# A hybrid conv and gating layer on one core: PE in the program's order, the convolution norm spread over the next units, the second half's input loaded later

## The chip, the core and the metric

The kernel runs on one core of a Trainium2 chip. The core has five engines with queues of their own: PE (TensorE, matrix products), DVE (VectorE), ACT (ScalarE), POOL (GpSimd) and SP (SyncE, which here only issues DMAs). ACT and POOL issue DMAs too, in line with their other work. The metric is the device time of one execution in microseconds.

## The reference

One layer on 2048 tokens of width 1024, in float32, cut to what matters here:

```python
h = rmsnorm(x, g_pre) * (1.0 + scale) + shift      # shift, scale, gate = c @ w_ada + b_ada
p = h @ w_in                                       # 8 column blocks of 1024
a = val * sigmoid(glu)                             # branch A
y = causal_depthwise_conv(a, conv_w, 31 taps) + conv_b
y = silu(layernorm(y, ln_g, ln_b)) * silu(z)       # norm over the 1024 channels
y_a = y @ w_conv_out
v = layernorm(gelu(v))                             # branch B
s = tril(w_s) mixes v in chunks of 128 positions, + bias
y_b = (gelu(u) * s * silu(z_b)) @ w_sgu_out
merged = sigmoid(g_a) * y_a + sigmoid(g_b) * y_b
out = rmsnorm(x + gate * (merged @ w_o), g_final)
```

## The kernel before, in words

The 2048 tokens are done in two halves of 1024 (`for s in range(NS)`, L590), each as two quarters of 512 tokens. Channels lie on the 128 partitions, tokens along the free dimension, except in the v pass and the last product, where it is the other way round. Every product with a weight matrix is made of three float32r matmuls, from operands split into a high and a low part (`split`, L84: an ACT copy gives the high part, a DVE or POOL subtraction the low one; `prod`, L289). Weight pieces are loaded by SP (`raw`), added up where needed and split, four pieces ahead of their use (`take`, L283).

The stages of a half:

- First half only: a part in which PE, DVE, ACT and POOL keep the program's order (`tc.manual_schedule(engines=MANUAL)`, L462 to L564). It computes the token rstd (column sums with `col_sums`, then `spread`), the conditioning `mod` from the wada loads (`ada`), and the first v pass. `load_xn(0, 1, xn)` (L528) loads the second quarter's tokens; wsT and sbias (L566 to L575) are the mixing weights and bias.
- The v pass of both quarters (`v_pass`, L443) with the position mixing (`mixing`, L422). Beside it `halves_sums` (L365) makes four sums or differences of the quarters per channel tile on DVE, which `split` turns into S1, S2, S4 and S3.
- 28 column groups (`quad`, L646). Each makes four blocks of two column tiles by two quarters with seven instead of eight products, of 12 matmuls each, in the order A11, A12, S1, S2, S4, S3, A22; A22 is put off until the next group's A11 is done (`pending`). Copies on ACT and subtractions on DVE link them: S4 adds to a bank that ACT has to copy first, A22 to one that DVE has to read first. Per channel tile there are three groups, for GLU (`glu`), for u and z (`uz`) and for the merge gates (`spilled`, Sigmoid); four more at the end (`spilled`, Silu) give the SiLU gate, stored to d_sz. The convolution of a tile (30 taps on DVE, `convolve`) is put in a list `bg`, and `run_bg(n)` takes n pieces from it at a lower priority.
- The product of branch B (`std_pairs(yb, done_b)`): 16 units of 24 matmuls. After each unit `done_b` multiplies the result with a loaded gate tile gl and stores it to d_mb. Between the units `run_bg(4)` takes four pieces: the token statistics of the next half (`token_stats`), and then the norm of the convolution: `mean` (two channel sums on PE), 16 steps of `centre` (two DVE operations and an ACT square), `ln_rstd` (column sums, root, `spread`, copy), and 16 steps of `conv_out` (scale, SiLU, times a loaded tile zl, split into ya).
- The product of branch A (`std_pairs(ya, done_a)`), which adds up the branches, and the output product (`out_half`, `finish_last`). In the first half the rstd spread and the inputs of the next half are made here, from `bg` (`next_rstd`, `make_h`).

Outside the manual part a scheduler lays out each engine's order ahead of time from its own model of the durations: it takes, of the instructions whose inputs are ready, the one with the lowest priority number, and the number grows along the program (`run_bg` adds LATER = 800). On the chip each engine then keeps that order. Tiles come from pools of fixed size: 28 large tiles (`hs`), six of 512 columns (`t512`), three for loads (`ld`: gl, zl, xs, rl, bl), six PSUM banks.

The change and the steps that speak of it touch the lines named here; the pieces of `bg` that it replaces are these:

```python
for h in range(2):
    bg.append(lambda h=h: mean(h))
for h in range(2):
    bg.extend(lambda h=h, j=j: centre(h, j) for j in range(KT))
    bg.append(lambda h=h: ln_rstd(h))
for h in range(2):
    bg.extend(lambda h=h, j=j: conv_out(h, j) for j in range(KT))
```

Of the kernel before, what the change touches and what calls it, by code (L numbers as in the profile page):

```python
# [7 lines left out]
F32 = mybir.dt.float32  # L8
F32R = mybir.dt.float32r
BF16 = mybir.dt.bfloat16  # L10
AF = mybir.ActivationFunctionType
# [9 lines left out]
T = 512  # L21
# [19 lines left out]
def hybrid_layer(  # L41
# [99 lines left out]
    def col_sums(val, pt, first, n):  # L141

        for c in range(n):
            nc.tensor.matmul(
                pt[:, first + c : first + c + 1], val[:, c * P : (c + 1) * P], one,
                start=True, stop=True,
            )
# [130 lines left out]
    def prep_to(n):  # L278
        while state["prep"] < min(n, len(order)):
            ready.append(order[state["prep"]]())  # L280
            state["prep"] += 1
# [82 lines left out]

    def halves_sums(xn, k):  # L365

        a11, a21 = xn[k][:, :T], xn[k][:, T:S]
        a12, a22 = xn[k + KH][:, :T], xn[k + KH][:, T:S]
        tt = nc.vector.tensor_tensor
        tt(out=a22, in0=a21, in1=a22, op=ALU.subtract)  # L370
        tt(out=a21, in0=a11, in1=a21, op=ALU.subtract)
        tt(out=a11, in0=a22, in1=a11, op=ALU.subtract)
        tt(out=a12, in0=a12, in1=a11, op=ALU.add)
        return a22, a11, a12, a21

# [86 lines left out]
    with tc.manual_schedule(engines=MANUAL):  # L462
# [20 lines left out]
        pc = bank()  # L483
        col_sums(acc, pc, 0, NC)
        prx = spread(rstd_cols(pc[:, :NC], NC), pc)
        rx = t512("rx")
# [15 lines left out]
        shifted(0)  # L502
        prep_to(2)
        cvt = wide()
# [9 lines left out]
        for k in range(KT):  # L514
# [6 lines left out]
            if k + 1 < KT:  # L521
# [4 lines left out]
                shifted(k + 1)  # L526
            if k == 2:
                load_xn(0, 1, xn)  # L528
            if k >= 4:
# [35 lines left out]

    wsT = row("wsT")  # L566
    nc.sync.dma_start(out=wsT, in_=wst.rearrange("p j t -> p (j t)"))
    sbias = hs32("sbias")
    nc.sync.dma_start(out=sbias, in_=rows[:, 2 * D : 3 * D].broadcast_to([P, D]))
    ws3 = wsT.rearrange("p (j t) -> p j t", t=P)  # L570
# [17 lines left out]

    gate_done = None
    for s in range(NS):  # L590
        last = s + 1 == NS
# [26 lines left out]

        pts = v_pass(A[1], mix_first)
        sums4 = [halves_sums(xn, k) for k in range(KH)]  # L620
        S1 = []
        for k in range(KH):
            S1.append(hs("s1"))
            split(S1[k], sums4[k][0])
        v_half(pts, vn1, st1, 1)
# [4 lines left out]
        rest = []  # L630
        for i in (1, 2, 3):
            group = []
            for k in range(KH):
                t = hs("s2")
                after(t[:, 0, 0:1], came)
                split(t, sums4[k][i])
                group.append(t)
            rest.append(group)
# [164 lines left out]

        for j in range(KT):
            glu(j)
            uz(j)
            spilled(AF.Sigmoid, d_sa[j], d_sbg[j])
        for i in range(KH):
            spilled(AF.Silu, d_sz[2 * i], d_sz[2 * i + 1])
        pending.pop()()  # L810
        run_bg(len(bg))


        yb = [[], []]
        for h in range(2):
            for j in range(KT):
                t = hs("yb")
                nc.sync.dma_start(
                    out=t.bitcast(F32).rearrange("p s c -> p (s c)"), in_=d_yb[j][h]
                )  # L820
                yb[h].append(t)

        pmu = []
        rsq = []
        ya = [[None] * KT, [None] * KT]

        def mean(h):
            pmu.append(sums(s1[0][:, h * T : (h + 1) * T]))

# [16 lines left out]

        def ln_rstd(h):
            hh = slice(h * T, (h + 1) * T)
            pc = bank()
            col_sums(rsq[0][:, hh], pc, 0, NC)  # L850
            pr = spread(rstd_cols(pc[:, :NC], NC), pc)
            nc.scalar.activation(rsq[0][:, hh], pr, AF.Copy)

# [9 lines left out]

        if not last:
            rs_next = []
            for h in range(2):
                ss, sq = token_stats(s + 1, h)
                bg.extend(sq)
                bg.append(lambda ss=ss, h=h: rs_next.append(token_rstd(ss, f"rsn{h}")))
        for h in range(2):  # L870
            bg.append(lambda h=h: mean(h))
        for h in range(2):
            bg.extend(lambda h=h, j=j: centre(h, j) for j in range(KT))
            bg.append(lambda h=h: ln_rstd(h))
        for h in range(2):
            bg.extend(lambda h=h, j=j: conv_out(h, j) for j in range(KT))

        def std_pairs(rhs, done):

            for q in range(4):  # L880
                ws = [[take(), take()] for _ in range(2)]
                for h in range(2):
                    for c in range(2):
                        pt = bank()
                        prod(pt, ws[c], rhs[h])
                        done(2 * q + c, h, pt)
                        run_bg(4)

        def done_b(j, h, pt):
            g = load(d_sbg[j][h], "gl")  # L890
            nc.vector.tensor_tensor(out=g, in0=pt, in1=g, op=ALU.mult)  # L891
            nc.gpsimd.dma_start(out=d_mb[j][h], in_=g)  # L892

        std_pairs(yb, done_b)
        run_bg(len(bg))

# [234 lines left out]
```

## Time and profile before

| what | us |
|---|---|
| median of 3 runs | 1947.18 (1946.78 to 1950.36) |
| the profiled execution, its own time | 1949.32 |
| its span, first to last instruction | 1947.6 |
| PE busy | 1859.1 (95%) |
| DVE busy | 1290.7 (66%) |
| ACT busy | 867.6 (45%) |
| POOL busy | 859.9 (44%) |

The mean granted clock of TensorE is 0.98 over the span. A busy share is a mean over stages with different limits; in the column groups PE is busy all the time, DVE mostly with taps and POOL with weights, and in the norm none of them is.

### The profile page before, as it was taken

The numbers are of one execution on the slowest core, as the hardware profiler recorded it, in microseconds if no ns is written. First come the engines' busy times: TensorE is split into PE (matmuls) and PEld (weight loads), VectorE is DVE, ScalarE is ACT, GpSimd is POOL, SyncE is SP. The second block draws the span as 40 slices with busy tenths as digits, with TensorE's granted clock in tenths as the row PEclk, the third lists the DMA queues.
The fourth block names the chain that finished last, engine by engine and source line by source line (L and its number), as shares of the span: only waits on it lengthen the run. The fifth ranks groups of instructions, "written<-read, shape, count | busy, mean of one in ns | idle before, by whom it ended". The sixth has DMA issues, their size and how long they took to land.

```text
span 1947.6 us, 23204 instructions
## 1 busy us (share of the span) xinstructions
PE 1859.1 (95%) x8116; PEld 1517.4 (78%) x8116; DVE 1290.7 (66%) x1636; ACT 867.6 (45%) x1396; POOL 859.9 (44%) x734
## 2 busy tenths in 40 slices
PE   6798999999999998889999999999999999899998
PEld 4577888888888886668888878888888888677886
DVE  6776898888888127475851578889888861845424
ACT  4645555555546435322611455554555453532102
POOL 0035777777777710000100477777777774000000
PEclk9899999999999998889999999999999999899999
DMA  9562332222334384387886332333322246536484
GB/s 331 174 238 92 109 114 100 101 87 92 114 103 146 132 328 137 107 292 243 330 308 220 120 141 75 105 114 103 114 92 97 77 141 253 173 111 198 132 331 169
DMA packets 139015, 313.66 MB, mean 161 GB/s; under 512 B 15889, under 2 KB 16017, under 8 KB 138898
## 3 DMA queue, kind: packets, MB, share of 16 engines
q1 hardware_dynamic: 108434, 237.03, 36.2%
q0 software_dynamic: 11888, 41.43, 5.5%
q10 hardware_dynamic: 18576, 33.73, 4.6%
q8 instruction: 63, 1.03, 0.2%
q14 instruction: 54, 0.44, 0.1%
HBM read 226.66 MB, written 85.46 MB: 160 GB/s over the span
## 4 chain that ended last, share of the span: by engine, by line
PE 74%; issue 11%; DMA 7%; DVE 4%; ACT 3%; POOL 2%; SPq 0%; POOLq 0%; ACTq 0%; DVEq 0%
PE bank L297 21%; PE bank L300 21%; PE bank L303 21%; PE bank L312 3%; PE bank L313 3%; PE bank L314 3%; DMA wo<-d_wo 1%; PE bank L426 1%; DVE wa L387 1%; POOL whl L88 1%; DMA raw<-in_w_v 1%; DMA wa<-in_wada 1%; DMA xn<-in_xt 1%; DMA whl<-d_wo 1%; POOL raw L224 1%
## 5 line engine op out<-in xcount | busy, mean ns | idle before, releaser
L88 POOL TENSOR_TENSOR whl<-raw,whl 128x512 fp32r<-128x512 f32 x392 | 512.8, 1313 | 335.3 <-ACT whl L87 331.1
L704 DVE SCALAR_TENSOR_TENSOR cv<-a,vec,cv 128x1024 f32<-128x1024 f32 x464 | 596.6, 1286 | 31.6 <-ACT cv L698 21.4
L87 ACT ACTIVATE whl<-raw 128x512 fp32r<-128x512 f32 x504 | 314.3, 627 | 414.1 <-PE bank L303 214.7
L300 PE MATMUL bank<-s,whl 128*128 128x512 f32 x896 | 349.3, 390 | 1.7 <-DVE s L88 1.7
L303 PE MATMUL bank<-s,whl 128*128 128x512 f32 x896 | 349.7, 390 | 0.0
L297 PE MATMUL bank<-s,whl 128*128 128x512 f32 x896 | 349.4, 390 | 0.0
L224 POOL TENSOR_TENSOR raw<-raw 128x512 f32<-128x512 f32 x224 | 290.3, 1296 | 17.2
L297 PE MATMUL bank<-h,whl 128*128 128x512 f32 x672 | 264.0, 393 | 0.3 <-ACT bank L657 0.2
L300 PE MATMUL bank<-h,whl 128*128 128x512 f32 x672 | 261.8, 390 | 0.0
L303 PE MATMUL bank<-h,whl 128*128 128x512 f32 x672 | 261.6, 389 | 0.0
L300 PEld LDWEIGHTS bank<-s,whl 128*128 128x128 f32 x896 | 168.6, 188 | 38.0 <-DVE s L88 3.0
L297 PEld LDWEIGHTS bank<-s,whl 128*128 128x128 f32 x896 | 168.6, 188 | 34.9
L303 PEld LDWEIGHTS bank<-s,whl 128*128 128x128 f32 x896 | 168.7, 188 | 34.7
L297 PEld LDWEIGHTS bank<-h,whl 128*128 128x128 f32 x672 | 126.1, 188 | 32.5 <-DVE snap L680 5.3
L303 PEld LDWEIGHTS bank<-h,whl 128*128 128x128 f32 x672 | 126.1, 188 | 26.5
L300 PEld LDWEIGHTS bank<-h,whl 128*128 128x128 f32 x672 | 126.2, 188 | 25.6
L88 DVE TENSOR_TENSOR whl<-raw,whl 128x512 fp32r<-128x512 f32 x112 | 75.9, 688 | 96.9 <-ACT whl L87 91.8
L892 POOL DMA_DIRECT2D mb<-gl x32 | 17.3, 541 | 275.0 <-DVE gl L891 264.3
L297 PE MATMUL bank<-ya,whl 128*128 128x512 f32 x256 | 102.6, 401 | 13.8 <-ACT ya L87 10.6
L652 ACT ACTIVATE snap<-bank 128x512 f32<-128x512 f32 x112 | 66.5, 598 | 98.0 <-PE bank L303 98.0
L297 PE MATMUL bank<-yb,whl 128*128 128x512 f32 x256 | 105.4, 412 | 4.2 <-DVE gl L891 3.5
L300 PE MATMUL bank<-ya,whl 128*128 128x512 f32 x256 | 102.6, 401 | 1.4 <-DVE ya L88 1.4
(214 smaller groups left out, 2867.3 us busy)
## 6 DMA issues: line engine op xcount, KB each, us to landing
raw<-in_w_in SPq DMA_DIRECT2D x224, 256.0 KB, 3.0
yb<-yb SPq DMA_DIRECT2D x32, 512.0 KB, 7.6
whl<-d_wo SPq DMA_DIRECT2D x32, 512.0 KB, 4.6
whl<-d_wv SPq DMA_DIRECT2D x32, 512.0 KB, 4.3
xn<-in_xt SPq DMA_DIRECT2D x32, 256.0 KB, 5.4
wa<-in_wada SPq DMA_DIRECT2D x16, 512.0 KB, 6.5
raw<-in_w_v SPq DMA_DIRECT2D x32, 256.0 KB, 4.8
d_wv<-whl POOLq DMA_DIRECT2D x16, 512.0 KB, 6.5
```

Of the source, the lines that this page charges most:

```text
L87: nc.scalar.activation(hi, val, AF.Copy)
L88: eng.tensor_tensor(out=lo, in0=val, in1=hi.bitcast(F32), op=ALU.subtract)
L224: eng.tensor_tensor(out=dst, in0=dst, in1=src, op=ALU.add)
L297: nc.tensor.matmul(pt, wh, h[:, 0], start=start and k == 0, stop=False, skip_group_check=True)
L300: nc.tensor.matmul(pt, wh, h[:, 1], start=False, stop=False, skip_group_check=True)
L303: nc.tensor.matmul(pt, wl, h[:, 0], start=False, stop=k == last, skip_group_check=True)
L312: nc.tensor.matmul(pt, xh, w[:, 0], start=kt == 0, stop=False)
L313: nc.tensor.matmul(pt, xh, w[:, 1], start=False, stop=False)
L314: nc.tensor.matmul(pt, xl, w[:, 0], start=False, stop=kt == KT - 1)
L387: nc.vector.tensor_tensor_reduce(out=wa[i], in0=wa[i], in1=cbc, scale=col(V_GPRE, k) if i else 1.0, scalar=0.0, op0=ALU.mult, op1=ALU.add, ...
L652: nc.scalar.activation(t, pt, AF.Copy)
L704: nc.vector.scalar_tensor_tensor(out=dst, in0=a[:, k : k + S], scalar=col(V_CW, j * TAPS + k), in1=cv[0], op0=ALU.mult, op1=ALU.add,)
```

## The change

It has four parts. From L590 on PE keeps the program's order, too (the other engines are still laid out by the scheduler). The norm of the convolution is no longer in `bg`: the channel sums and all centring steps stand before the last column group (`before_last`), and column sums, spreads and `conv_out` steps stand behind numbered units of branch B's product (`steps`: unit 4q + 2h + c). The second quarter's tokens, wsT and sbias are loaded only after a one-column copy from `mod` into their tiles (`after`), and the first two weight pieces are made ahead of the first spread. The sums of the quarters are made one by one, where each is split, instead of all ahead of S1.

```diff
-    def halves_sums(xn, k):
...
+    def quarters(xn, k):
+        return xn[k][:, :T], xn[k + KH][:, :T], xn[k][:, T:S], xn[k + KH][:, T:S]
+
+    def sum1(xn, k):
+
+        a11, a12, a21, a22 = quarters(xn, k)
+        nc.vector.tensor_tensor(out=a22, in0=a21, in1=a22, op=ALU.subtract)
+        return a22
+
+    def sum2(xn, k):
+        a11, a12, a21, a22 = quarters(xn, k)
+        nc.vector.tensor_tensor(out=a21, in0=a11, in1=a21, op=ALU.subtract)
+        nc.vector.tensor_tensor(out=a11, in0=a22, in1=a11, op=ALU.subtract)
+        return a11
+
+    def sum4(xn, k):
+        a11, a12, a21, a22 = quarters(xn, k)
+        nc.vector.tensor_tensor(out=a12, in0=a12, in1=a11, op=ALU.add)
+        return a12
+
+    def sum3(xn, k):
+        return quarters(xn, k)[2]
...
         col_sums(acc, pc, 0, NC)
+        prep_to(2)
         prx = spread(rstd_cols(pc[:, :NC], NC), pc)
...
         shifted(0)
-        prep_to(2)
...
             if k == 2:
+                for i in range(KT):
+                    after(xn[i][:, T : T + 1], mod[:, 3, 0:1])
                 load_xn(0, 1, xn)
...
     wsT = row("wsT")
+    after(wsT[:, 0:1], mod[:, KT - 1, 0:1])
     nc.sync.dma_start(out=wsT, in_=wst.rearrange("p j t -> p (j t)"))
     sbias = hs32("sbias")
+    after(sbias[:, 0:1], mod[:, KT - 1, 0:1])
     nc.sync.dma_start(out=sbias, in_=rows[:, 2 * D : 3 * D].broadcast_to([P, D]))
...
     gate_done = None
+    ctx.enter_context(tc.manual_schedule(engines={ET.PE}))
     for s in range(NS):
...
-        sums4 = [halves_sums(xn, k) for k in range(KH)]
         S1 = []
         for k in range(KH):
             S1.append(hs("s1"))
-            split(S1[k], sums4[k][0])
+            split(S1[k], sum1(xn, k))
...
-        for i in (1, 2, 3):
+        for sum_of in (sum2, sum4, sum3):
             group = []
             for k in range(KH):
                 t = hs("s2")
                 after(t[:, 0, 0:1], came)
-                split(t, sums4[k][i])
+                split(t, sum_of(xn, k))
...
+        def before_last():
+            for h in range(2):
+                pmu.append(sums(s1[0][:, h * T : (h + 1) * T]))
+            for h in range(2):
+                for j in range(KT):
+                    centre(h, j)
...
-        def ln_rstd(h):
-            hh = slice(h * T, (h + 1) * T)
+        def ln_cols(h):
             pc = bank()
-            col_sums(rsq[0][:, hh], pc, 0, NC)
-            pr = spread(rstd_cols(pc[:, :NC], NC), pc)
-            nc.scalar.activation(rsq[0][:, hh], pr, AF.Copy)
+            col_sums(rsq[0][:, h * T : (h + 1) * T], pc, 0, NC)
+            ln_pc.append((pc, rstd_cols(pc[:, :NC], NC)))
+
+        def ln_spread(h):
+            pc, cols = ln_pc[h]
+            pr = spread(cols, pc)
+            nc.scalar.activation(rsq[0][:, h * T : (h + 1) * T], pr, AF.Copy)
...
+        steps = {
+            1: [lambda: ln_cols(0)], 2: [lambda: ln_spread(0)],
+            3: [lambda: ln_cols(1)], 4: [lambda: ln_spread(1)],
+        }
+        for j in range(KT):
+            steps.setdefault(3 + j, []).append(lambda j=j: conv_out(0, j))
+            steps.setdefault(8 + j, []).append(lambda j=j: conv_out(1, j))
...
         for i in range(KH):
+            if i == KH - 1:
+                run_bg(len(bg))
+                before_last()
             spilled(AF.Silu, d_sz[2 * i], d_sz[2 * i + 1])
         pending.pop()()
         run_bg(len(bg))
...
                         done(2 * q + c, h, pt)
                         run_bg(4)
+                        for step in steps.pop(4 * q + 2 * h + c, ()):
+                            step()
```

What is not shown: the loads of yb stand behind the definitions now, and the token statistics go into `bg` behind them, as its only pieces.

## Rows read from the trace of the kernel before

**Rows 1.** The page, part 1: busy us, share of the span, instructions.

```profile
PE 1859.1 (95%) x8116; PEld 1517.4 (78%) x8116; DVE 1290.7 (66%) x1636; ACT 867.6 (45%) x1396; POOL 859.9 (44%) x734
```

**Rows 2.** PE by stretches: stretch, its length, busy (matmuls), granted clock, DMA share, GB/s.

```profile
200.00:600.00 400.00, 400.00 (x1762) 1.00 0.30 102
722.00:880.00 158.00, 131.68 (x524) 0.89 0.57 183
1655.00:1762.00 107.00, 94.22 (x386) 0.92 0.46 153
```

**Rows 3.** The same two stretches, matmuls that read yb alone.

```profile
722.00:880.00 158.00, 68.50 (x281) 0.89 0.57 183
1655.00:1762.00 107.00, 89.30 (x362) 0.92 0.46 153
```

**Rows 4.** Groups on PE from 722 to 880: count, busy us, mean ns, idle before.

```profile
L144 PE MATMUL bank<-one,rsq 128*128 128x1 f32 x16 | 2.5, 261 | 8.3 <-DVE rsq L843 8.3
L161 PE MATMUL bank<-diag,ones 128*128 128x512 f32 x4 | 2.2, 630 | 2.8 <-ACT q L842 1.4 <-DVE diag L154 1.4
L166 PE MATMUL bank<-s,ones 128*128 128x512 f32 x4 | 1.9, 591 | 0.0
```

**Rows 5.** Waits of PE from 722 to 880: us in total, times, longest.

```profile
PE bank L297 <- ACT ya L87: 10.6, 2, 5.5
PE bank L144 <- DVE rsq L843: 8.3, 2, 6.2
...
PE bank L297 <- DVE gl L891: 1.2, 1, 1.2
```

**Rows 6.** One stretch, all engines: PE, PEld, DVE, ACT, POOL busy, clock, DMA.

```profile
646.00:700.00 54.00, 54.00 (x240) 44.47 (x239) 6.91 (x10) 24.46 (x42) 30.62 (x24) 1.00 0.62 233
```

**Rows 7.** Groups on DVE from 730 to 850: the adding up of squares.

```profile
L843 DVE TENSOR_TENSOR rsq<-rsq,q 128x512 f32<-128x512 f32 x14 | 9.6, 683 | 0.9 <-ACT q L842 0.7
```

**Rows 8.** Timeline of PE and DVE near 695: start us, us, what.

```profile
695.28 0.39 PE L303 MATMUL bank<-s,whl 128*128 128x512 f32 x1
...
695.71 0.69 DVE L680 TENSOR_TENSOR snap<-snap,bank 128x512 f32<-128x512 f32 x1 [1.31 <-PE bank L303]
```

**Rows 9.** Timeline of DVE and POOL near 176.

```profile
175.58 2.78 DVE L88 TENSOR_TENSOR s<-xn,s 128x512 fp32r<-128x512 f32 x2
...
176.51 1.29 POOL L88 TENSOR_TENSOR whl<-raw,whl 128x512 fp32r<-128x512 f32 x1
```

**Rows 10.** Timeline of ACT, PE and DVE in the start.

```profile
20.21 0.81 ACT L352 ACTIVATE h<-xn,mod 128x512 fp32r<-128x512 f32 x1 [0.76 <-DVE xn L492]
...
22.44 0.79 PE L539 MATMUL bank<-whl,h 128*128 128x512 f32 x1 [3.62 <-ACT whl L87]
...
58.69 1.23 DVE L387 CUSTOM_DVE_ANT_0 wa<-wa,cbc 128x1024 f32<-128x1024 f32 x1 [4.02 <-DMA wa<-in_wada]
```

**Rows 11.** Timeline of PE in the v pass.

```profile
108.39 0.50 PE L313 MATMUL bank<-whl,h 128*128 128x512 f32 x1 [2.01 <-DVE whl L88]
```

**Rows 12.** Timeline of PE and ACT in one group of the merge gates.

```profile
326.51 0.39 PE L303 MATMUL bank<-s,whl 128*128 128x512 f32 x1
...
326.72 0.59 ACT L652 ACTIVATE snap<-bank 128x512 f32<-128x512 f32 x1
...
328.55 0.39 PE L297 MATMUL bank<-s,whl 128*128 128x512 f32 x1
```

**Rows 13.** Timeline of PE and DVE where the output product begins.

```profile
918.75 0.80 PE L312 MATMUL bank<-whl,mg 128*128 128x512 f32 x1
...
924.63 0.68 DVE L154 TENSOR_TENSOR diag<-ident,rsn 128x512 f32<-128x512 f32 x1
```

**Rows 14.** DMA issues from 690 to 850: count, KB each, median us to landing.

```profile
mb<-gl POOLq DMA_DIRECT2D x16, 256.0 KB, 3.6
zl<-sz SPq DMA_DIRECT2D x16, 256.0 KB, 2.9
gl<-sbg SPq DMA_DIRECT2D x13, 256.0 KB, 2.8
```

More of the change, by code (lines that the diff above doesn't have):

```diff
@@ L363, in make_h @@
         A[h].append(t)
-    def halves_sums(xn, k):
[L367 to L374, printed above, removed]
+    def quarters(xn, k):
[15 more added lines that the diff above has]
+        return quarters(xn, k)[2]
     def load_ada(k):
@@ L802, in spilled @@
             )
[L804 to L821, printed above, removed]
         pmu = []
@@ L825, in hybrid_layer @@
         ya = [[None] * KT, [None] * KT]
-        def mean(h):
-            pmu.append(sums(s1[0][:, h * T : (h + 1) * T]))
+        ln_pc = []
+        def before_last():
[4 more added lines that the diff above has]
+                    centre(h, j)
         def centre(h, j):
@@ L862, in conv_out @@
             split(ya[h][j], v)
[L864 to L869, printed above, removed]
-        for h in range(2):
[L871 to L876, printed above, removed]
+        steps = {
[5 more added lines that the diff above has]
+            steps.setdefault(8 + j, []).append(lambda j=j: conv_out(1, j))
+        for j in range(KT):
+            glu(j)
+            uz(j)
+            spilled(AF.Sigmoid, d_sa[j], d_sbg[j])
+        for i in range(KH):
+            if i == KH - 1:
+                run_bg(len(bg))
+                before_last()
+            spilled(AF.Silu, d_sz[2 * i], d_sz[2 * i + 1])
+        pending.pop()()
+        run_bg(len(bg))
+        yb = [[], []]
+        for h in range(2):
+            for j in range(KT):
+                t = hs("yb")
+                nc.sync.dma_start(
+                    out=t.bitcast(F32).rearrange("p s c -> p (s c)"), in_=d_yb[j][h]
+                )
+                yb[h].append(t)
         def std_pairs(rhs, done):
@@ L892, in done_b @@
             nc.gpsimd.dma_start(out=d_mb[j][h], in_=g)
+        if not last:
+            rs_next = []
+            for h in range(2):
+                ss, sq = token_stats(s + 1, h)
+                bg.extend(sq)
+                bg.append(lambda ss=ss, h=h: rs_next.append(token_rstd(ss, f"rsn{h}")))
         std_pairs(yb, done_b)
```

## The prediction

> **What bounds the kernel now.** I read the page first: PE is busy 95% of the span [rows 1], so only time in which PE stands still, or runs at its lower clock, can be won. Then PE by stretches [rows 2]: in the column groups from 200 to 600 us it starts 1762 matmuls in 400 us, 0.227 us apart, at a full granted clock. Two stretches are worse: 722 to 880 us, where the convolution norm of the first half lies among the output products, and 1655 to 1762 us, the same place in the second half. Their granted clock is 0.89 and 0.92, between the levels 2.4 GHz (1.00) and 1.2 GHz (0.50), because PE ran part of them at the lower one.
>
> What these stretches cost: the first holds 524 matmuls [rows 2], of which 24 are small work of the norm (16 column sums, 4 spreads, 4 sums of channels) [rows 4] and 500 are products of two units' inputs, 281 of them from yb [rows 3]. 500 x 0.227 = 113.5 us, so 158.0 - 113.5 = **44.5 us** are not product time. The second has 362 yb products [rows 3]: 107.0 - 82.2 = **24.8 us**. The small matmuls themselves are busy 2.5 + 2.2 + 1.9 = 6.6 us [rows 4]. The largest waits say who is late: the first ya tile's copy by ACT, 10.6 us, and the squares' sum on DVE, 8.3 us [rows 5]. The norm is late, not PE.
>
> **Part 1: the norm placed unit by unit.** The two channel sums and all 16 centring steps move ahead of the last column group. Their input is there: between 646 and 700 us DVE is busy 6.9 of 54 us [rows 6], so the taps have ended. A centring step is two DVE operations and one ACT square; a DVE one takes 0.683 us [rows 7], so 16 x 2 x 0.683 = 22 us on DVE, beside the last group's 84 x 0.227 = 19 us of PE. The norm's column sums stand behind units 1 and 3 of yb, the spreads behind units 2 and 4, and a unit is 24 x 0.227 = 5.4 us: the last square sum is due about 22 us after the last group ends, so it is hidden. conv_out (three DVE operations, 2.05 us; two on ACT) comes once a unit, twice in units 8 to 10. With done_b and one weight split that is at most 4.1 + 1.4 = 5.5 us of DVE against 5.4: hidden, without slack in three units. Its zl loads move with it on SP's queue, between the gl loads; in the first half the token statistics' xs loads come behind the yb loads as before.
>
> What stays of 44.5 and 24.8: the 6.6 us of small matmuls in each. New in each: in the program's order the last group's A22 product stands straight behind S3, and it waits for a DVE subtraction; S3's last matmul is over at 695.28 + 0.23, the subtraction at 695.71 + 0.69 [rows 8], so 0.9 us, where four yb products filled the gap. A centring step ahead of it on DVE adds 0.7: I take 1.5. For loads and splits that come late I estimate 3.5 us in the first half and 2.0 in the second (bounds 0, and 15 and 10 if the waits for rsq stay [rows 5]). So 11.6 and 10.1 us stay, and 32.9 + 14.7 = **47.6 us** go.
>
> On that subtraction a row speaks against the move: two DVE splits with both inputs in SBUF took 2.78 us at 175.58, where two take 1.37 by [rows 7], while POOL ran its own at 176.51 [rows 9]. The Trainium skill has the rule (SBUF — State Buffer, "Who interferes with whom"): a DVE instruction with two SBUF inputs and a GpSimd one that reads SBUF block each other for a whole instruction. By it the square sums, now beside POOL's splits of the last group, could put one such block of 1.4 us ahead of the subtraction in each half, and the sum would give 44.8 instead of 47.6; I leave it in the range.
>
> **Part 2: input and sums made later.** The first weight splits move ahead of the spread. PE starts its products at 22.44 us after a wait of 3.62 for the split; ACT's h is done at 20.21 + 0.81 = 21.02 [rows 10], so 1.4 us go. The second half's eight xn loads leave their early place on SP's queue for one behind mod[3]; what stands behind them there are the weights' and wada's loads of the next steps, and eight one-column copies (under 0.15 us each) enter DVE's chain. Early wada loads gain, later ones lose; the wait of 4.0 us at 58.69 for a wada load [rows 10] is not touched. wsT and sbias load after mod[7], with their mask and copies on POOL behind; they are wanted after 128 us. Net **1.5 us** (bounds -4 and +6). The quarter sums leave DVE where it makes PE wait 2.0 us for a weight split at 108.39 [rows 11]; they run in later DVE gaps: **1.0** (bounds 0 and 2, or a loss of 2 if S2 then waits).
>
> **Part 3: PE in the program's order.** 40 of the 56 column groups have that order already, counted in PE's timeline. In 16 groups (8 in each half, those of the merge gates), the old order put matmuls of the next group ahead of S4, mostly 8 [rows 12]: S2 ends at 326.51 + 0.23 and S4 starts at 328.55. In the new order S4 waits there for ACT's copy of its bank, done at 326.72 + 0.59 = 327.31, 0.6 us; everything behind S4 on PE waits too. 16 x 0.6 = 9.6 us (bounds 0, if ACT's order shifts, and 16 x 8 x 0.227 = 29). In the first group of each half the old order filled waits with 15 such matmuls (3 and 12), 3.4 us; I take half, 2 x 1.7 = 3.4 (bounds 0 and 6.8). The rstd spread for the next half moves to behind the first weight tile of out_half: PE is there at 918.75 + 12 x 0.227 = 921.5, the DVE product it needs ends at 924.63 + 0.68 = 925.3 [rows 13], 3.8 us; I take 4 (bounds 1 and 6). Sum **17.0 us** lost.
>
> **Sum.** 47.6 + 1.5 + 1.0 - 17.0 = 33.1. The profiled execution took 1949.3 us (span 1947.6 and 1.7 around it), so 1916.2; the median shown is 2.1 lower, so **1914 us**. A measurement tells about 0.2%, 4 us, from no change.
>
> **Rivals.**
> *Order free.* ACT's order is laid out anew, and S4 never waits: part 3 costs 17.0 - 9.6 - 1.4 = 6, so 1903. For it: 40 groups run so. Against: the copy comes behind ACT's work on the group before, in either order. Chance 0.20.
> *Order in full.* Every matmul that filled a gap covered a real wait: 29 + 6.8 + 6 = 42 instead of 17, so 1939. For it: the gaps were filled where something was expected late. Against: the ACT copy ends after 0.6 us. Chance 0.13.
> *Norm half won.* DVE's queue keeps centring steps and late loads in an order in which PE still waits for rsq: 24 of 47.6, so 1938. For it: the old order expected the squares' sum earlier than it came [rows 5]. Chance 0.13.
> *Slower: the three load tiles bind.* gl, zl and xs share three buffers. A gl tile is held for 2.8 (load) + 0.7 + 0.5 + 3.6 us (store) = 7.6, a zl tile for 2.9 + 2.2 = 5.1 [rows 14]; 16 of each, and 8 xs held like a zl tile (they are read by one ACT operation), make 244 tile-us in the first half, 203 in the second, against 3 x 87 = 261 in a yb pass. It fits, but not if tiles are fetched ahead: x us more for each of the 32 tiles lengthens the passes by (64x - 75)/3, which eats the 33 us at x = 2.7. At x = 4 it is 60 us: 1974. Against: with the same tiles in use, PE waited 1.2 us for gl and 10.6 for ya [rows 5]. Chance 0.06.
> *Forecast* 0.44; 0.04 for the rest (a slower start, more won).
>
> **How the numbers follow.** 1914 is the likeliest case; its own range, from its bounds, is 1904 to 1927. Order free reaches down to 1897, the two at 1938 and 1939 stay in up to 1942; load tiles and tails are left out: **1897 to 1942**. Faster holds all but the load tiles, and small parts of the tails: 0.88, same 0.05, slower 0.07.
>
> **What would show it.** Right: channel sums before the last group's first product, PE's waits for rsq and for ya's copy gone, the two stretches' surplus near 11 us, a PE wait of about 0.6 us before S4 in 16 groups with no matmuls of the next group ahead of it, and one of about 4 us in out_half. Wrong: idle time of PE for gl or for a split during yb (load tiles), a DVE subtraction late by several us in the last group, or a wada wait that grew in the first 80 us.

## The result and the profile after

The changed kernel took 1961.89 us (median, 1959.48 to 1966.23); the kernel before, on the same chip, 1947.26. The ratio is 1.0074, 95% interval [1.0053, 1.0096]: slower by 14.6 us, where 1914 had been forecast, with a range that ended at 1942.

The page of the changed kernel, span and part 1, against [rows 1]:

```profile
span 1957.8 us, 23201 instructions
...
PE 1860.5 (95%) x8116; PEld 1515.8 (77%) x8116; DVE 1300.1 (66%) x1646; ACT 871.6 (45%) x1396; POOL 866.8 (44%) x734
```

The same work on every engine (DVE has ten one-column copies more), in a span 10.2 us longer. That is less than the 14.6 us of the medians: the profiled execution of the kernel before took 1949.32 us and that of the changed one 1959.48, the shortest of its four. Where the time went is read best by stages. A stage ends where PE starts the first product of the next one in the timeline, the last one with PE's last product (7.5 us before the end of the span in both); lengths in us:

| stage | before | after | difference |
|---|---|---|---|
| start, up to the first column group | 148.0 | 155.0 | +7.0 |
| column groups, first half | 547.5 | 575.8 | +28.3 |
| products of yb and ya (the norm), first half | 222.0 | 189.3 | -32.7 |
| output, and v pass of the second half | 185.4 | 191.3 | +5.9 |
| column groups, second half | 545.0 | 567.3 | +22.3 |
| products of yb and ya, second half | 202.6 | 177.9 | -24.7 |
| output of the second half | 89.6 | 93.8 | +4.2 |

In the kernel before, the first products of yb stand ahead of A22, so A22's 12 x 0.227 = 2.7 us count there with the norm and in the changed kernel with the groups. Moved over, the norm's stages gained 30.0 + 22.0 = **52.0 us** and the groups lost 25.6 + 19.6 = **45.2 us**. The rest lost 17.1.

PE by stretches of the changed kernel: a stretch inside the groups, then the two stages of [rows 2] (the second one up to the first ya product). Columns: length, then busy and matmuls of PE, PEld, DVE, ACT and POOL, then granted clock, DMA share, GB/s.

```profile
200.00:600.00 400.00, 396.78 (x1743) 326.38 (x1742) 332.55 (x318) 210.03 (x331) 299.21 (x230) 1.00 0.30 100
730.80:920.00 189.20, 182.38 (x790) 148.02 (x789) 104.83 (x171) 63.17 (x106) 10.83 (x20) 0.98 0.67 219
1678.60:1769.30 90.70, 90.70 (x405) 74.61 (x404) 52.77 (x83) 38.50 (x57) 8.15 (x15) 1.00 0.55 180
```

The granted clock, 0.89 and 0.92 before, is 0.98 and 1.00: the norm's stages are cured. But the groups, which never stood still in [rows 2], now have 1743 matmuls where they had 1762. The waits of PE in the changed kernel say on what (line, releaser: us in total, times, longest):

```profile
PE bank L297 <- ACT snap L668: 23.7, 18, 7.8
PE bank L553 <- ACT h L352: 10.8, 3, 8.2
...
PE bank L161 <- DVE diag L154: 6.5, 2, 3.3
PE bank L297 <- ACT whl L87: 5.8, 3, 4.5
PE bank L297 <- DVE snap L696: 3.9, 3, 2.3
PE bank L312 <- DMA wo<-d_wo: 3.3, 6, 1.5
```

The waits for `rsq` and `ya` of [rows 5] are gone. In their place stand ACT's copy of a bank (`snap`), the modulated tiles of the start (`h`, 4.5 us before), and smaller ones for a spread (`diag`, one in the start and one in the output), for weight splits (`whl`, in the product of branch A) and for the output weights (`wo`).

**The longest copy wait.** Timeline of PE, ACT and DVE in the last group of the first half, changed kernel (start us, us, what, idle before):

```profile
711.35 0.39 PE L303 MATMUL bank<-s,whl 128*128 128x512 f32 x1
719.55 0.80 PE L297 MATMUL bank<-s,whl 128*128 128x512 f32 x1 [7.81 <-ACT snap L668]
...
715.66 0.63 ACT L845 ACTIVATE q<-a 128x512 f32<-128x512 f32 x1 [0.57 <-DVE a L838]
716.86 0.63 ACT L845 ACTIVATE q<-a 128x512 f32<-128x512 f32 x1 [0.57 <-DVE a L838]
717.39 1.07 ACT L804 ACTIVATE sp<-bank 128x512 f32<-128x512 f32 x2
...
718.90 1.08 ACT L668 ACTIVATE snap<-bank 128x512 f32<-128x512 f32 x2 [0.44 <-ACT sp L804]
...
716.09 0.68 DVE L838 SCALAR_TENSOR_TENSOR a<-bank,a 128x512 f32<-128x512 f32 x1
```

S2 ends at 711.6 and S4 waits for the copy of the bank it writes to. That copy stands on ACT behind all sixteen squares of the centring, and each square waits for a DVE subtraction; subtractions and additions take turns on DVE, a pair every 1.2 us. So the copy comes only when the whole chain has run. The second half shows the same wait, 7.8 us at 1666.

**The start.** Timeline of SP's DMA issues, DVE and PE, changed kernel:

```profile
35.00 0.42 SPq L393 DMA_DIRECT2D wa<-in_wada  x1
40.27 5.08 SPq L329 DMA_DIRECT2D xn<-in_xt  x8
45.40 0.59 SPq L393 DMA_DIRECT2D wa<-in_wada  x1
...
40.10 0.57 DVE L92 COPY xn<-mod 128x1 f32<-128x1 f32 x8
...
52.88 1.28 DVE L399 CUSTOM_DVE_ANT_0 wa<-wa,cbc,vec 128x1024 f32<-128x1024 f32 x1 [9.75 <-DMA wa<-in_wada]
...
55.28 0.79 PE L553 MATMUL bank<-whl,h 128*128 128x512 f32 x1 [8.18 <-ACT h L352]
```

The eight loads are those of the second quarter's tokens, `load_xn(0, 1, xn)`; the title, the prediction and some of the expectations call them the second half's input. They wait for the fourth shift and then go out in one piece, between the two tiles of one `wada` pair. Wait of SP's queue from 30 to 50 us:

```profile
SPq L329 <- DVE xn L92: 5.1, 1, 5.1
```

So the held loads kept the queue standing for 5.1 us, with the second `wada` tile in line behind them, and then took 5.1 us to issue. That tile is issued 10 us after the first, and DVE waits 9.75 us for it, where the longest such wait was 4.02 [rows 10].

### The profile page after: what moved, and what is told of

It reads as the page before. It is cut to its first block, busy times and chain, and to the rows that moved or that the text cites. A ratio compares the mean times of both kernels' runs of the same rounds, so it can differ in the third digit from the quotient of the medians.

```text
span 1957.8 us, 23201 instructions
## 1 busy us (share of the span) xinstructions
PE 1860.5 (95%) x8116; PEld 1515.8 (77%) x8116; DVE 1300.1 (66%) x1646; ACT 871.6 (45%) x1396; POOL 866.8 (44%) x734
## 4 chain that ended last, share of the span: by engine, by line
PE 72%; issue 9%; DMA 7%; ACT 5%; DVE 5%; POOL 2%; SPq 0%; ACTq 0%; POOLq 0%; DVEq 0%
PE bank L297 20%; PE bank L303 20%; PE bank L300 20%; PE bank L312 3%; PE bank L314 3%; PE bank L313 3%; DMA wo<-d_wo 1%; PE bank L438 1%; ACT whl L87 1%; ACT L804 1%; DMA zl<-sz 1%; DVE wa L399 1%; DVE cv L720 1%; DMA wa<-in_wada 1%; POOL whl L88 1%
## 5 line engine op out<-in xcount | busy, mean ns | idle before, releaser
L88 POOL TENSOR_TENSOR whl<-raw,whl 128x512 fp32r<-128x512 f32 x392 | 518.6, 1326 | 351.4 <-ACT whl L87 344.1
L720 DVE SCALAR_TENSOR_TENSOR cv<-a,vec,cv 128x1024 f32<-128x1024 f32 x464 | 596.8, 1286 | 31.5 <-ACT cv L714 21.4
L297 PE MATMUL bank<-ya,whl 128*128 128x512 f32 x256 | 101.0, 395 | 5.8 <-ACT whl L87 5.8
L303 PE MATMUL bank<-ya,whl 128*128 128x512 f32 x256 | 101.1, 395 | 1.1 <-DVE whl L88 0.9
L300 PE MATMUL bank<-ya,whl 128*128 128x512 f32 x256 | 100.6, 393 | 0.0
```

What stands on the lines that cost most here:

```text
L88: eng.tensor_tensor(out=lo, in0=val, in1=hi.bitcast(F32), op=ALU.subtract)
L297: nc.tensor.matmul(pt, wh, h[:, 0], start=start and k == 0, stop=False, skip_group_check=True)
L300: nc.tensor.matmul(pt, wh, h[:, 1], start=False, stop=False, skip_group_check=True)
L303: nc.tensor.matmul(pt, wl, h[:, 0], start=False, stop=k == last, skip_group_check=True)
L720: nc.vector.scalar_tensor_tensor(out=dst, in0=a[:, k : k + S], scalar=col(V_CW, j * TAPS + k), in1=cv[0], op0=ALU.mult, op1=ALU.add,)
```

## The experiments

All times are medians; the ratio is to the kernel before, run beside them: 1948.23 us for experiments 1 to 4, 1948.47 for 5 to 8, 1949.24 for 9 to 12. By the intervals of the ratios, a difference between two of these kernels is known to 4 or 5 us. Stages are those of one profiled execution, which can lie 2 us off the median.

**1. The centring in the queue of small steps.**

```diff
 def before_last():
     for h in range(2):
         pmu.append(sums(s1[0][:, h * T : (h + 1) * T]))
     for h in range(2):
-        for j in range(KT):
-            centre(h, j)
+        bg.extend(lambda h=h, j=j: centre(h, j) for j in range(KT))
```

> The changed kernel, with the sixteen centring steps of the convolution norm handed to the queue of small steps (two after each product, the rest behind the last group) where the change issues all of them ahead of the last group; PE's order and all else are as changed. Theory: the two waits of 7.8 us for the copies at L668, with the slower clock behind each, come from fourteen squares that stand ahead of the copy on ScalarE, each waiting for a VectorE subtraction; last group and A22 go from 33.3 and 34.1 us back to 24 to 25, so 14 to 20 us less than the 1961.9 of the changed kernel: 1942 to 1948, likeliest 1945, and the longest wait for a copy is below 2 us. Rival: VectorE's work in the last group is too much in whatever order; the wait turns up at the first products of yb instead (on the norm's sums and its spread), and the gain is 0 to 7 us: 1955 to 1962.

Measured: **1945.9 us**, ratio to before 0.9993 [0.9977, 1.0009]; 16.0 us less than the changed kernel. Waits of PE in this kernel:

```profile
PE bank L297 <- ACT snap L668: 8.3, 16, 1.4
```

The long waits are gone and did not come back at yb; the theory holds. (It is sixteen squares, not fourteen.) So the centring's place cost 8 us in each half. The sixteen short waits in the groups are left.

**2. The changed kernel without the order on PE.**

```diff
-    ctx.enter_context(tc.manual_schedule(engines={ET.PE}))
```

> The changed kernel without the line that holds PE to the program's order; all else as changed. Theory: the order costs what the trace of the changed kernel shows on PE, 0.62 us in each of the sixteen groups and 2 to 4 us in each mixing, first group and output stage, 24 us in all, and outside the order PE also fills part of the two long waits of the last group with products of yb: 22 to 36 us less than 1961.9, so 1926 to 1940, likeliest 1932. Rival: the norm gains only because its small products are held to their units; let free, they stand again where an estimate puts them and the waits for rsq and ya come back, as in the kernel before: 1945 to 1960.

Measured: **1922.34 us**, 0.9872 [0.9851, 0.9892]: 39.6 us less than the changed kernel, a little beyond the theory's 22 to 36. The rival is out: the norm's small products stay with their units and no wait for `rsq` or `ya` returns. The centring still shows; timeline of PE and DVE behind the last group:

```profile
697.71 0.40 PE L300 MATMUL bank<-yb,whl 128*128 128x512 f32 x1
703.33 0.80 PE L303 MATMUL bank<-yb,whl 128*128 128x512 f32 x1 [5.22 <-DVE whl L88]
...
702.00 0.68 DVE L845 TENSOR_TENSOR rsq<-rsq,q 128x512 f32<-128x512 f32 x1
702.60 0.68 DVE L88 TENSOR_TENSOR whl<-raw,whl 128x512 fp32r<-128x512 f32 x1
```

PE passes S4 and goes on to yb, and stops there on a weight split that stands behind the same chain on DVE.

**3. The start as before, in the changed kernel.**

```diff
-        prep_to(2)
         prx = spread(rstd_cols(pc[:, :NC], NC), pc)
...
         shifted(0)
+        prep_to(2)
...
-                for i in range(KT):
-                    after(xn[i][:, T : T + 1], mod[:, 3, 0:1])
...
-    after(wsT[:, 0:1], mod[:, KT - 1, 0:1])
...
-    after(sbias[:, 0:1], mod[:, KT - 1, 0:1])
```

> The changed kernel with the edits to the start undone: no waits ahead of the second half's input, the triangle of weights or the bias, and the first weight split back in its place. Theory: the second half's input, held until the fourth shift is known, then goes to the queue as one burst ahead of a later tile of the modulation's weights, which lands 9.75 us after VectorE asks for it (before: 4.0); undone, the start is 4 to 7 us shorter: 1955 to 1958. Rival: the start is bound by the sum of what it has to load, and a later stage takes up the time: 0 to 2 us, 1960 to 1962.

Measured: **1955.68 us**, 1.0041 [1.0026, 1.0057]: 6.2 us less than the changed kernel, as the theory had it.

**4. The order alone, in the kernel before.**

```diff
     gate_done = None
+    ctx.enter_context(tc.manual_schedule(engines={ET.PE}))
     for s in range(NS):
```

> The kernel before, with nothing added but the line that holds PE to the program's order behind the start. Theory: the groups lose 12 to 14 us in the first half of the sequence and 6 in the second, the output stage 5, and the norm, whose small products are then in line behind VectorE's chain, 0 to 10 more than before: 20 to 35 us slower than 1947.3, so 1967 to 1982. Rival: the waits that the changed kernel's groups show come from its later sums of quarters and from the norm, not from the order: 1947 to 1957.

Measured: **1947.19 us**, 0.9996 [0.9983, 1.0009]: no change. My theory failed here, and its rival's reason fails too, for the stages moved a lot, in both directions: groups +16.4 and +10.8 us, output +7.5 and +6.9, norm **-29.6 and -15.4** (2.7 of each pair is A22, moved over). So the order by itself wins 39.6 us in the norm's stages, and loses as much elsewhere. Why is in the timeline of DVE and PE of the kernel before:

```profile
767.50 0.68 DVE L843 TENSOR_TENSOR rsq<-rsq,q 128x512 f32<-128x512 f32 x1
...
768.24 0.58 PE L144 MATMUL bank<-one,rsq 128*128 128x1 f32 x2 [6.19 <-DVE rsq L843]
...
814.54 0.72 PE L144 MATMUL bank<-one,rsq 128*128 128x1 f32 x6
```

and in the same two engines of this kernel:

```profile
771.57 0.69 DVE L844 TENSOR_TENSOR rsq<-rsq,q 128x512 f32<-128x512 f32 x1
...
778.65 0.95 PE L144 MATMUL bank<-one,rsq 128*128 128x1 f32 x8
```

In both the last sum of squares of the second tile is done by 768 and 772. The program's order takes the eight column sums at 778.65; PE's free order had put two of the eight ahead of their data, where PE stood 6.19 us of the 8.3 for `rsq` [rows 5], and six at 814.54, 46 us behind their data. Spread, multiplication and ya stood behind these: the 10.6 us wait for `ya` [rows 5] was a wait for PE's own late products.

**5. Order, start and centring undone together; the norm's units and the later sums of quarters stay.** The diffs of 1, 2 and 3 in one kernel.

> The changed kernel with three things undone together: no line for PE's order, the start as before, and the centring steps of the convolution norm in the queue of small steps in place of ahead of the last group. What is left of the change is the norm's placing unit by unit and the later sums of quarters. Theory: the three costs are apart from each other. From 1922.3 without the order, 6 us less for the start, and per half 6 to 8 us less for the wait of 5.22 us on a weight split behind the centring on VectorE and for the slower clock behind it: 1898 to 1906, likeliest 1903. Rival: without the order PE already passes what the centring holds up, and the wait only moves on to the norm's sums: 1912 to 1918.

Measured: **1902.12 us**, 0.9763 [0.975, 0.9776]. Theory right; this beats both kernels. Its page and the waits of PE inside the first yb and ya stage:

```profile
PE 1843.8 (97%) x8116; PEld 1508.4 (79%) x8116; DVE 1296.7 (68%) x1636; ACT 864.8 (46%) x1396; POOL 859.4 (45%) x734
```

```profile
PE bank L297 <- ACT whl L87: 4.6, 2, 4.0
PE bank L297 <- DVE snap L691: 1.4, 1, 1.4
PE bank L303 <- DVE xn L92: 0.7, 1, 0.7
```

**6. The same, with the centring ahead of the last group again** (the diff of 1 taken back).

> As the kernel beside it that undoes order, start and centring, but with the centring ahead of the last group as the change has it. Theory: 1922.3 less 6 for the start: 1914 to 1918, and 11 to 16 us behind the kernel beside it. Rival: centring ahead costs only under PE's order: within 3 us of the kernel beside it.

Measured: **1915.94 us**, 0.9832 [0.9819, 0.9845]: 13.8 us behind kernel 5. The centring's place costs under either order, 16.0 with it (experiment 1) and 13.8 without.

**7. Kernel 5 with the sums of quarters at once, as before.**

```diff
+        sums4 = [halves_sums(xn, k) for k in range(KH)]
         S1 = []
...
-            split(S1[k], sum1(xn, k))
+            split(S1[k], sums4[k][0])
...
-        for sum_of in (sum2, sum4, sum3):
+        for i in (1, 2, 3):
...
-                split(t, sum_of(xn, k))
+                split(t, sums4[k][i])
```

> As the kernel that undoes order, start and centring, with the sums of quarters too made at once as before. Theory: the prediction took 1.0 us for making them later; within 2 us of the kernel beside it, on either side. Rival: the sums at once hold VectorE and with it the first products of the groups: 3 to 8 us slower.

Measured: **1903.87 us**, 0.9773 [0.9758, 0.9787], against 0.9763 [0.975, 0.9776]: no difference that these runs can tell. This part is worth 1.8 us at the medians, if anything.

**8. The kernel before with the order over yb and ya alone.**

```diff
-        std_pairs(yb, done_b)
-        run_bg(len(bg))
+        with tc.manual_schedule(engines={ET.PE}):
+            std_pairs(yb, done_b)
+            run_bg(len(bg))
...
-        std_pairs(ya, done_a)
-        run_bg(len(bg))
+        with tc.manual_schedule(engines={ET.PE}):
+            std_pairs(ya, done_a)
+            run_bg(len(bg))
```

> The kernel before, with PE held to the program's order over the products of yb and ya alone, in both halves; groups, mixing, output and start stay free. Theory: the norm's surplus came from where PE's free order put the small products, and either cure takes the whole of it: over these stages the kernel with the order everywhere showed 192.4 us for 222.0 and 187.2 for 202.6, so 45 us less than 1947.3 without the losses elsewhere: 1900 to 1908. Rival: the order's losses elsewhere are the price of the same thing, PE's work being moved across stages, and held here it shows up in the stages beside: 1930 to 1947.

Measured: **1917.88 us**, 0.983 [0.9812, 0.9848]. Between the two: 30.6 us won, two thirds of what I expected. The norm's stages are 199.2 and 190.9 us, 22.8 and 11.7 less than before, 10.5 short of the 45: 5.4 are A22, which counts with the norm here and which I had missed. The first half's output stage is 3.8 us longer. The waits of PE in this kernel show what the placing unit by unit gives beyond the order:

```profile
PE bank L161 <- DVE diag L154: 13.3, 5, 5.1
```

In the old program the spread stands right behind its column sums and PE waits for DVE's diagonal; with a unit's product between the two, kernel 5 shows 1.5 us for all of its spreads, all of it in the start. That is 11.8 of the 15.8 us between kernels 8 and 5.

**9. Kernel 5 with the order over the column groups alone**, and **10. the same with S1's product ahead of A12's.** The edit of 9, then that of 10:

```diff
+        in_order = tc.manual_schedule(engines={ET.PE})
+        in_order.__enter__()
         for j in range(KT):
             glu(j)
...
         pending.pop()()
         run_bg(len(bg))
+        in_order.__exit__(None, None, None)
```

```diff
-            prod(a, [take()], A12, start=False)
-            c11(a)
-            run_bg(2)
             c = bank()
             prod(c, [take()], S1)
             p5 = snap(c)
             run_bg(2)
+            prod(a, [take()], A12, start=False)
+            c11(a)
+            run_bg(2)
...
-            order += [quad_piece(q, k) for k in ("b21", "t1", "t2", "b22", "t3")]
+            order += [quad_piece(q, k) for k in ("t1", "b21", "t2", "b22", "t3")]
```

> The kernel of 1902 us, which undoes order, start and centring, with PE held to the program's order over the column groups alone (mixing of the second tile included). Theory: the order's price lies first in the groups; there the two traces that differ by order and start show 564.5 us for 549.2 in the first half and 560.2 for 547.2 in the second, 28 us, of which 8 are products of yb that the free order had drawn ahead: 1918 to 1931, likeliest 1922. Rival: the prediction's price, sixteen waits of 0.6 us and 3 us for the first group of each half: 1911 to 1917.

> As the kernel beside it with the groups in order, and the product of the first sums (S1) written before that of A12 in each group, so that the copy of its bank has a product more before S4 writes there. Theory: it is not order as such that costs, but this order, in which S4 waits in sixteen groups for a copy that stands behind ScalarE's work for the group before; written so, these waits go: 8 to 14 us less than the kernel beside it. Rival: the wait moves to the next product that needs ScalarE or VectorE in the same group, and nothing is won: within 3 us.

Measured: 9 took **1923.49 us**, 0.9871 [0.985, 0.9892], 21.4 us more than kernel 5; 10 took **1907.97 us**, 0.9797 [0.9777, 0.9818], 15.5 us less than 9. The theory of 9 holds; that of 10 holds in kind, with a gain 1.5 us above its 8 to 14. Waits of PE in 9:

```profile
PE bank L297 <- ACT snap L663: 8.4, 17, 0.8
```

In 10 the copies have no row among PE's waits any more; the largest of its groups' waits is for splits of the sums, of which S1's are wanted one product earlier:

```profile
PE bank L300 <- DVE s L88: 9.1, 11, 2.8
```

So most of the price in the groups is that of one place in the written order, not of an order as such. The 15.5 us are more than the sixteen waits (9.9 us, below): by stages the groups win 14.4 us in the first half and 4.7 in the second, and the norm's stages lose 2.9 and 2.8 of it again. What else is won in the first half's groups was not taken apart.

**11. Kernel 5 with the order over the output stages alone.**

```diff
+        in_order = tc.manual_schedule(engines={ET.PE})
+        in_order.__enter__()
         came = mg[1][KT - 1][:, 1, 0:1].bitcast(F32)
...
         out_half(0)
         out_half(1)
+        in_order.__exit__(None, None, None)
```

The exit stands behind the last half's output too.

> The kernel of 1902 us with PE held to the program's order over the output stages alone (from the merge's end on, in both halves). Theory: this stage pays 7 us in the first half (spread of the next tokens' factor in line behind a VectorE step) and 7 at the end (late output weights, which PE may not pass): 1913 to 1918. Rival: the prediction's 4.0 us for this stage and nothing at the end: 1905 to 1907.

Measured: **1919.06 us**, 0.9848 [0.9826, 0.987]: 17.0 us more, 1 above the theory's range. By stages the first half's output takes 6.4 us more and the last output 8.0, 14.4 in all; the profiled execution is 19.0 us longer than kernel 5's, and the other 4.6 lie in stages that the edit does not touch. Waits of PE in this kernel:

```profile
PE bank L312 <- DMA wo<-d_wo: 4.4, 8, 1.5
...
PE bank L161 <- DVE rx L92: 3.6, 1, 3.6
```

The free order fills the time in which the output weights arrive (0.3 us of such waits in kernel 5); in order, each late tile stops PE.

**12. Kernel 5 with the hold on the second quarter's tokens alone.**

```diff
             if k == 2:
+                for i in range(KT):
+                    after(xn[i][:, T : T + 1], mod[:, 3, 0:1])
                 load_xn(0, 1, xn)
```

> The kernel of 1902 us with one edit of the start put back: the second half's input waits for the fourth shift of the modulation. Theory: this edit alone makes the start longer, by the modulation weights that come behind the burst: 4 to 7 us more, 1906 to 1909. Rival: it is the first weight split, put ahead of the spread of the token factor, or the later triangle and bias, and the hold costs nothing: 1901 to 1904.

Measured: **1910.03 us**, 0.9802 [0.978, 0.9823]: 7.9 us more, 1 above the theory's range. The line of the `wada` reductions (idle time before them), in kernel 5 and then here:

```profile
DMA wa<-in_wada: 6.5, 3
```

```profile
DMA wa<-in_wada: 13.6, 3
```

DVE waits 7.1 us more. The profiled execution is 10.3 us longer than kernel 5's: the start 4.5, the rest in later stages (mostly the first half's norm and output, 2.9 and 2.6), which was not followed further. In the profiled executions with the hold the start takes 152.3 to 158.0 us; in those without it 147.6 to 149.2, but 151.8 in experiment 3. So the hold alone costs as much as all edits of the start together (6.2 to 6.4), as far as these runs can tell.

## Why the prediction was wrong, point by point

Three steps failed: what the centring ahead of the last group costs, what the held loads cost, and the sum of what the order costs. The parts add up. From kernel 5, by its own median: 1902.1, + 13.8 for the centring's place (6), + 6.4 for the start (experiment 2 less 6), + 21.4 and + 17.0 for the order in groups and output (9, 11) make 1960.7; the changed kernel took 1961.9. As each part is known to 4 or 5 us, that it comes out within 1.2 is partly chance.

| part | forecast, us | measured, us | from |
|---|---|---|---|
| norm unit by unit and sums of quarters | -51.6 | -46.3 | kernel 5 against before |
| centring ahead of the last group | +3.0 | +13.8 to +16.0 | 6, 1 |
| start | -1.5 | +6.2 to +6.4 | 3, 2 less 6 |
| order, column groups | +13.0 | +21.4 | 9 |
| order, output | +4.0 | +17.0 (14.4 in its own stages) | 11 |

(The forecast's -47.6 held 1.5 us of loss in each last group; they stand in a row of their own here, and its 1.0 for the sums with the first row.)

**Part 1, the gain: right in size, wrong in cause.** The norm's waits went, and the channel sums stand ahead of the last group's first product. The size was worked out from the surplus of the stretches, so it did not hang on the cause; of its estimate for late loads and splits (3.5 and 2.0 us) the first half shows 6.7 us of PE waiting for weight splits, the second none. But "The norm is late, not PE" was wrong: the sums of squares were done at 768, and PE's free order took their columns at 814 (experiment 4). The prediction read the releaser of ya's wait, ACT, and did not follow it back to PE. Had it done so, it could have seen that the order alone cures most of the same loss (39.6 us, experiment 4). The change pays for two cures of one loss: on the kernel before, the order wins about 40 us in the norm and loses as much elsewhere; beside the norm's units it wins next to nothing, and costs 38 to 40.

**Part 1, the failed step: "A centring step ahead of it on DVE adds 0.7: I take 1.5".** The 22 us of DVE were laid beside 19 us of PE and taken as hidden. They were not beside it but in line: the sixteen squares stand on ACT ahead of the group's copies, and S4 waits for the copy. The step looked at A22, behind S3, and at DVE alone; the wait came two products earlier, on ACT. It is 7.8 us in each half, and 8 us in each by experiment 1. The prediction's list of signs had it ("a DVE subtraction late by several us in the last group"), its sum had not.

**Part 2, the failed step: "Early wada loads gain, later ones lose", with a net gain of 1.5 us and a loss of at most 4.** The prediction saw that the loads behind the moved ones are those of `wada`, and then took the gain of the first split as the likelier end. The hold kept SP's queue standing for 5.1 us and then made 2 MB (eight tiles of 256 KB) one burst, both ahead of a tile that was needed 3 us after the burst began. The wait at 58.69 that it named did stay (3.07 us in the changed kernel); a new one of 9.75 us came ahead of it. The loss of 6.2 to 6.4 us is over the bound of 4. Of the split's 1.4 us nothing came: the first product starts at 23.2 us, not earlier than 22.44 [rows 10]. Moved ahead of the spread, the split's two ACT copies, and a table load of 1.28 us behind them, stand before the root of the token rstd, which starts at 17.44 us where it started at 15.36:

```profile
14.81 1.32 ACT L87 ACTIVATE whl<-raw 128x512 fp32r<-128x512 f32 x2 [2.58 <-DMA raw<-in_w_v]
...
17.44 0.26 ACT L137 ACTIVATE cols<-bank,eps_t 128x4 f32<-128x4 f32 x1
```

**Part 3: the price of one wait right, the sum too small.** S4's wait is as forecast, 0.62 us of lost pitch, 0.46 of it the wait, in each of the groups of the merge gates but the last (16 x 0.62 = 9.9 us):

```profile
222.81 0.59 ACT L668 ACTIVATE snap<-bank 128x512 f32<-128x512 f32 x1
...
223.45 0.50 PE L297 MATMUL bank<-s,whl 128*128 128x512 f32 x1 [0.46 <-ACT snap L668]
```

The eight matmuls of the next group that stood there before [rows 12] are gone. The failed step is "Sum 17.0 us lost": what was mis-sized is all else. The other half of the 21.4, where 3.4 stood, lies nearly all in the first half, whose groups are 14.8 us longer in kernel 9 than in kernel 5 (5.5 in the second half). There PE waits in the first group for splits of the sums (0.58, 1.13 and 1.25 us) and runs behind these waits at a granted clock of 0.52 from 184 to 188 us, where kernel 5 has 1.00. The output cost 17.0, where 4.0 stood for one spread, which alone measured 3.2 us in the changed kernel:

```profile
927.70 1.44 PE L161 MATMUL bank<-diag,ones 128*128 128x512 f32 x2 [3.16 <-DVE diag L154]
```

The last output, where PE may no longer pass late weights, had no term at all. The rival *order in full* (42 us, against 38 to 40) had the size by luck, for another reason: matmuls that filled gaps in the groups.

**The sum.** Short were the gain by 5.3, the centring by 10.8, the start by 7.9, the order by 8.4 in the groups and 13.0 in the output: 45.4 us, and with the 1.3 by which the kernel before stood higher in these runs, 1914 becomes 1960.7. The range took the misses one at a time; five on the same side were in no case of it. The slower rival named the load tiles, and PE's waits in the products of yb and ya show none for them.

**The rule on DVE and GpSimd, weighed in the prediction.** In the last group of the first half four additions of squares took longer than the usual 0.68 us, beside POOL's work. Timeline of DVE and POOL, changed kernel:

```profile
704.01 1.18 DVE L846 TENSOR_TENSOR rsq<-rsq,q 128x512 f32<-128x512 f32 x1
...
707.42 1.54 DVE L846 TENSOR_TENSOR rsq<-rsq,q 128x512 f32<-128x512 f32 x1
...
702.95 3.39 POOL L88 TENSOR_TENSOR whl<-raw,whl 128x512 fp32r<-128x512 f32 x2 [2.41 <-ACT whl L87]
707.12 1.30 POOL L88 TENSOR_TENSOR whl<-raw,whl 128x512 fp32r<-128x512 f32 x1 [0.78 <-ACT whl L87]
```

With two more of 1.14 and 1.18 us that makes 2.3 us in a chain of 20; the second half shows the same four. By the Trainium skill (SBUF — State Buffer, "Who interferes with whom") such pairs block each other. The trace agrees, and POOL's two splits took 3.39 us where two take 2.6. It is at most 2.3 us of each 7.8, where the prediction had weighed 1.4 in each half.

## What to carry to other kernels

A step moved ahead of a critical stage is not hidden because its engine time fits beside that stage: write down what stands behind it on each in-order engine, ACT as well as DVE, and when PE needs that. Before two cures are added up, follow the wait back to its first cause; here both removed the same loss, and only one of them had a price elsewhere. A held load also holds what stands behind it in its queue, and is a burst when it is let go: look at what is next there.

## What was not expected of the hardware

After a wait of 7.8 us PE comes back at its lower clock. Stretches of the changed kernel before and behind S4's start (length, busy of each engine, granted clock, DMA share, GB/s):

```profile
700.00:711.00 11.00, 11.00 (x50) 9.11 (x49) 11.00 (x15) 6.99 (x13) 5.23 (x4) 1.00 0.87 322
719.50:723.50 4.00, 3.95 (x9) 3.14 (x10) 0.00 (x0) 0.48 (x1) 0.00 (x0) 0.50 1.03 405
724.00:727.00 3.00, 3.00 (x14) 2.25 (x12) 1.35 (x2) 1.26 (x2) 0.00 (x0) 1.00 0.77 285
```

Granted clock 1.00 (2.4 GHz), 0.50 (1.2 GHz) for nine matmuls, then 1.00 again: 9 matmuls in 4.0 us where 2.0 would do, so 2 us on top of the wait. In the second half, behind the wait of 7.76 us, it was at least 13 matmuls at 0.50 (1666.4 to 1672.0 us). A wait of 0.46 us in the groups had no such tail. The prediction priced waits without it.
